# A fused two-block kernel: the shift of the last feed-forward stage taken out of the matmuls and summed on VectorE in the stage before

## The chip, the cores and the metric

The kernel runs as one program on one core of a Trainium2 chip. The metric is the device time of one execution in microseconds (us). A profile is one execution taken by the hardware profiler; its times start at the first instruction.

## The reference, cut to what matters

Two transformer blocks follow each other. The second has two layers over a context of 256 tokens and a latent of 512 tokens, width 1024, with a modulation computed from a condition vector. Only the end of its second layer is touched:

```
def modulate(x, g, shift, scale):
    return rmsnorm_2(x, g) * (1 + scale) + shift

def swiglu(h, w_in, w_out):
    g, u = jnp.split(h @ w_in, 2, axis=-1)
    return (jax.nn.silu(g) * u) @ w_out
...
x = x + g2 * rmsnorm_2(swiglu(modulate(x, norm_g[l, 2], sh2, sc2), ffn_w_in[l], ffn_w_out[l]), norm_g[l, 3])
```

`w_in` is 1024 x 5632 (22 groups of 128 gate columns and 22 of up columns, D_FF_2 = 2816), `w_out` 2816 x 1024. Everything is float32. For l = 1 (the last layer) only the 512 latent tokens are computed here. Since a norm's factor is one number per token, `modulate(x) @ w` is `r * ((x * g * (1 + scale)) @ w) + shift @ w`: the last term is one number per output row, the same for all tokens. The kernel works with it in this form.

## The kernel before, in words

Activations lie transposed: 128 channels on the partitions, tokens along the free axis. A float32 product is made of three fp32r matmuls, high x high, low x high and high x low parts, so every operand is split into a `hi` copy (ScalarE, L306) and a `lo` rest (VectorE, L307). `wload` fetches 128 x 1024 weights (512 KB) on SyncE's queue into one of three `raw` buffers (L303) and splits them into one of two `whi`/`wlo` pairs; it is written 300 places ahead of where it stands (`ahead`), so that weights come early.

`proj2` makes one projection: 8 steps k over the 1024 input channels, in each the three products for each segment of columns (`mm2`, matmul on L1020). The normalized but unscaled activations are in `hh` (hi) and `hl` (lo), [128, 8, 832] each. In a segment of 258 columns two columns hold the shift of latent and context: their product is `shift @ w`, which `ffn2` copies out of PSUM (L1656, L1664, 128 x 2) and adds as the bias of Silu (L355) and in L1669.

`ffn2(0, ...)`, called the first feed-forward stage below (layer 0, about 1737 to 2260 us), works on 768 tokens in segments of 258 and 512 columns. `ffn2(1, ...)`, the last one (about 2555 to 2912 us), works on 512 tokens in segments of 258 (`segl`: shift columns and latent tokens 0 to 255) and 256 columns. Either has 22 units of a gate and an up projection. The first two projections are made by `first2` (L980) in pieces while the stage before still ends, so 42 are left. Groups of 2, 4, 4, 4, 4 and 4 units are followed by their share of `w_out` (output tiles d, pairs of them in one weight load, 512 columns in one pass for the last stage); the last group is done by `sums` (L1616), 256 columns at a time, followed by `post`, which normalizes, adds the residual and stores.

The order on TensorE is the order in which the program is written. The other engines' order is laid out by a planner before the run. `tick` is called after each step k of a projection and each hidden tile of a down product; it advances side work (generators put in with `later`), which is how work is spread among the matmuls. Earlier, `ada_steps` already does such side work: it fetches 128 x 512 pieces (256 KB, tile `araw`, three buffers) during the first block's feed-forward stages and multiplies and sums each with two condition vectors in VectorE instructions with an accumulator (L869).

`lt`/`LT`/`LTB` say at which column of `hh` the latent tokens begin: 320 until the attention of layer 1, then 304. The arena of a stage has a fixed number of tile slots (`t`, 128 x 768): 25 in the first stage, 26 in the last.

Of the kernel before, what the change touches and what calls it, by code (L numbers as in the profile page):

```python
# [9 lines left out]
F32 = mybir.dt.float32  # L10
# [3 lines left out]
ALU = mybir.AluOpType  # L14
AX = mybir.AxisListType
PSUM = bass.MemoryType.PSUM

P = 128
S = 512
SC = 256  # L20
T2 = S + SC


CO, LT, HW = 16, 320, 832
LTB = 304
KD = 8
NF = 22
EPS = 1e-6
WU = 1024
# [125 lines left out]
def _pack_second(i):  # L155
    a = {}
    a["ctxT"] = np.ascontiguousarray(i["ctx_2"][0].T)

    a["ada"] = np.ascontiguousarray(i["ada_w_2"].transpose(0, 2, 1)).reshape(-1)
    a["cond"] = np.stack([i["c_2"][0], i["c_ctx_2"]])  # L160
    w = _Units("w2")
    wi = i["ab_w_in_2"][0]
    gc = [-1] * P
    for n, o in ((0, 0), (2, 32), (1, 64), (3, 96)):
        gc[o:o + 4] = _rng(4096 + 4 * n, 4)
    w.add("bg", _units(wi, [gc]))
    for h in range(4):
        w.add(("hg", h), _units(wi, [_rng(1536 + h * P), _rng(2048 + h * P), _rng(h * P), _rng(512 + h * P)]))
    w.add("bqk", _units(wi, [_rng(2560 + j * P) for j in range(4)]))
    w.add("bv", _units(wi, [_rng(3072 + h * P) for h in range(4)]))  # L170
    w.add("gate", _units(wi, [_rng(1024 + h * P) for h in range(4)] + [_rng(3584 + h * P) for h in range(4)]))
    w.add("abo", _units(i["ab_w_out_2"][0], [_rng(d * P) for d in range(KD)]))

    def ffn(l):
        wf = i["ffn_w_in_2"][l]
        _ffn(w, l, wf[:, :NF * P], wf[:, NF * P:], i["ffn_w_out_2"][l])

    ffn(0)
    perm = np.concatenate([np.arange(32), np.arange(64, 96), np.arange(32, 64), np.arange(96, P)])
    wq = i["attn_w_qkv_2"][0]  # L180
    w.add("ck", _units(wq, [8 * P + perm, 9 * P + perm]))
    w.add("cv", _units(wq, [_rng(10 * P), _rng(11 * P)]))
    w.add("cq", _units(wq, [h * P + perm for h in range(8)]))
    w.add("co", _units(i["attn_w_out_2"][0], [_rng(d * P) for d in range(KD)]))
    ffn(1)
    a["w2"] = w.array()
    gb = np.zeros((P, 1), np.float32)
    for n, o in ((0, 0), (2, 32), (1, 64), (3, 96)):
        gb[o:o + 4, 0] = i["ab_gate_b_2"][0, n]
    v = [_cols(i["ada_b_2"][l]) for l in range(2)]  # L190
    v += [_cols(i["norm_g_2"][l, n]) for l in range(2) for n in range(4)]
    v += [_cols(i["ab_conv_2"][0, n]) for n in range(3)]
    v += [gb]
    v += [_cols(i["hgrn_lb_2"][d, n]) for d in range(2) for n in range(3)]
    v += [_cols(i["ab_out_g_2"][0])]
    v += [_cols(i["attn_qk_g_2"][0, n][perm]) for n in range(2)]
    a["vec2"] = np.concatenate(v, axis=1)
    return a
# [61 lines left out]
class Body:  # L260
# [643 lines left out]
    def shift2(self, l, m, ctx=True, lat=False):  # L904

        sh = self.ada[l][:, m * 8:m * 8 + 8, :]
        for o in (CO + SC,) * ctx + (self.lt - 2,) * lat:
            self.split(self.hh[:, :, o:o + 2], self.hl[:, :, o:o + 2], sh)

    def squares2(self, k, x, o, w, acc, tmp=None):  # L910

# [12 lines left out]
    def feed2(self, k, x, o, w, l, n):  # L924

        for c, s in ((0, 1), (SC, 0)):
            a, b = max(o, c), min(o + w, (SC, T2)[1 - s])
            if a < b:
                h = a + (self.lt - SC, CO)[s]
                self.split_scaled(self.hh[:, k, h:h + b - a], self.hl[:, k, h:h + b - a], x[:, a - o:b - o],  # L930
                                  self.mod[l][n][:, k, s:s + 1])

# [12 lines left out]

    SEG = ((CO, SC + 2), (LT, S))

    @property
    def segl(self):
        return ((self.lt - 2, SC + 2), (self.lt + SC, SC))  # L950

    @property
    def partl(self):
        return ((0, 0, self.lt - 2, SC + 2), (1, 0, self.lt + SC, SC))

    def proj2(self, seg, key, u=0):

        if self.pre:
            return self.pre.pop(0)
        ps = self.mmtile()  # L960
        wh, wl = self.wload("w2", key, u)
        self.mm2(ps, wh, wl, 0, [(self.hh[:, k, :], self.hl[:, k, :]) for k in range(KD)], seg)
        return ps

    PART = ((0, 0, CO, SC + 2), (1, 0, LT, SC), (1, SC, LT + SC, SC))

    def first2(self, parts, units, pend):
# [670 lines left out]
    def ffn2(self, l, r, seg, lat, parts, acc, post):  # L1638

        nc = self.nc  # L1640
        ys = [None] * KD
        if lat:
            cols = ((slice(SC, 2 * SC), 0, 2, 0), (slice(2 * SC, T2), 1, 0, 0))
            bcol = slice(0, 2)
            hseg, outs = ((SC, S),), ((slice(SC, T2), 0),)
        else:
            cols = ((slice(0, SC), 0, 0, 1), (slice(SC, T2), 1, 0, 0))
            bcol = slice(SC, SC + 2)
            hseg, outs = self.SEGM, ((slice(0, SC), 0), (slice(SC, T2), 1))
        hid = []  # L1650

        def unit(f):
            pg = self.proj2(seg, ("f", l, f), 0)
            a = self.T()
            bg = self.small(2)
            nc.vector.tensor_copy(bg, pg[:, 0, bcol])  # L1656
            for c, b, p0, s in cols:
                n = c.stop - c.start
                nc.vector.tensor_tensor(a[:, c], pg[:, b, p0:p0 + n], r[:, c], ALU.mult)
                self.act(a[:, c], a[:, c], AF.Silu, bias=bg[:, s:s + 1])  # L1660
            pu = self.proj2(seg, ("f", l, f), 1)
            u = self.T()
            bu = self.small(2)
            nc.vector.tensor_copy(bu, pu[:, 0, bcol])  # L1664
            hi, lo = self.T(F32R), self.T(F32R)
            for c, b, p0, s in cols:
                n = c.stop - c.start
                nc.vector.tensor_tensor(u[:, c], pu[:, b, p0:p0 + n], r[:, c], ALU.mult)
                nc.vector.scalar_tensor_tensor(a[:, c], u[:, c], bu[:, s:s + 1], a[:, c], ALU.add, ALU.mult)  # L1669
                self.split(hi[:, c], lo[:, c], a[:, c])  # L1670
            hid.append((hi, lo, 0, 0))

        f = 0
        for gi, g in enumerate(GROUPS):
# [6 lines left out]
            for d in range(0, KD, 2):  # L1681
                wh, wl = self.wload("w2", ("d", l, gi), d // 2, 2 * g * P)
                for i in range(2):
                    ps = self.mmtile() if len(hseg) > 1 else Banks(self.aux())
                    self.mm2(ps, wh, wl, i * g * P, hid[:g], hseg)
                    k = d + i
# [8 lines left out]
            del hid[:g]  # L1695
        if not lat:
            self.shift2(1, 0, lat=True)
        W = []
        for o, w in parts:
            for d in range(0, KD, 2):  # L1700
# [16 lines left out]
    def mixer_c(self, r):  # L1717
        nc = self.nc
# [72 lines left out]
            lag(rest)  # L1791

        def qproj(h):
            ps = self.proj2(self.segl, "cq", h)
            z = T()
            b = self.small(2)
            nc.vector.tensor_copy(b, ps[:, 0, 0:2])
            nc.vector.tensor_tensor(z[:, :SC], ps[:, 0, 2:SC + 2], r[:, SC:2 * SC], ALU.mult)
            nc.vector.tensor_tensor(z[:, SC:], ps[:, 1, :SC], r[:, 2 * SC:T2], ALU.mult)
            nc.scalar.activation(z, z, AF.Identity, bias=b[:, 0:1])  # L1800
            sqs = squares(z, S)
            hi, lo = T(F32R), T(F32R)
            qs.append((hi, lo))

            def rest():
                headnorm(z, sqs, S, 0)
                rope(z)
                self.split(hi, lo, z)
            lag(rest)
# [4 lines left out]
        held = []  # L1814

        def store(h, o):
            hc = slice(LTB, LTB + S)
            self.split(self.hh[:, h, hc], self.hl[:, h, hc], o)

        def attend(h, qp):  # L1820
# [54 lines left out]
        for n in range(2 * 16 + 4):  # L1875
# [7 lines left out]
                store(*held.pop(0))  # L1883
            if n == 1 or n % 4 == 0 and 0 < n <= 20:
                late.pop(0)()
        return [(self.hh[:, h, :], self.hl[:, h, :], CO, LTB - SC) for h in range(8)]

    def arena(self, name, slots, width=784):
        es = ExitStack()
# [5 lines left out]
    def second_begin(self):  # L1895

        nc, tc = self.nc, self.tc
        self.e2 = ExitStack()
        pb = self.e2.enter_context(tc.tile_pool(name="blk2", bufs=1, reuse_waits="tile"))
        self.dr = self.e2.enter_context(tc.tile_pool(name="dram", bufs=1, space=bass.MemoryType.DRAM))  # L1900
        self.lt = LT
        self.hh = pb.tile([P, KD, HW], F32R, tag="hh", name="hh")
        self.hl = pb.tile([P, KD, HW], F32R, tag="hl", name="hl")
        self.accs = [pb.tile([P, T2], F32, tag=f"acc{i}", name=f"acc2{i}") for i in range(2)]
# [1 line left out]
        p = es.enter_context(tc.tile_pool(name="ctx0", bufs=1, reuse_waits="tile"))  # L1906
# [9 lines left out]
    def second(self, xall, pf, hb, acc, ef, eb):  # L1916

        nc, tc = self.nc, self.tc
# [14 lines left out]
        def leave(o, tail):  # L1933
            c = slice(o, o + SC)
            v, r = self.stats1(pf, acc, c, tail)
            for k in range(KD):
# [38 lines left out]
        self.drain()  # L1975
        ea.close()

        ea = self.arena("ffn20", 25, T2)
        self.ffn2(0, n0, self.SEG, False, ((0, SC), (SC, SC), (S, SC)), na,
                  lambda ys, o, w: self.post(ys, 0, o, w, na, self.mod[0][3], feed(1, 0), n0))  # L1980
        self.first2(self.PART, (("ck", 0), ("ck", 1)), norms)
# [4 lines left out]

        ea = self.arena("mixc", 20, S)
        mix = self.mixer_c(n0)
        self.lt = LTB
        self.lo_eng = nc.vector  # L1990
        ea.close()

        ex = self.residual(SC)
        nc.sync.dma_start(self.xr, spill[1])
        ea = self.arena("out1", 14, T2)
        self.shift2(1, 3, ctx=False, lat=True)
        self.out2("co", mix, ((SC, SC), (S, SC)), SC, na,
                  lambda ys, o, w: self.post(ys, SC, o, w, na, self.mod[1][1], feed(1, 2), n0))
        self.first2(self.partl, ((("f", 1, 0), 0), (("f", 1, 0), 1)), norms[1:])
        self.drain()  # L2000
        ea.close()

# [2 lines left out]
        def store(k, x, o, w):  # L2005
            if k % 2:
# [1 line left out]
                dst = self.out[(k - 1) * P:(k + 1) * P, o - SC:o - SC + w]  # L2008
                nc.sync.dma_start(dst.rearrange("(k p) s -> p k s", p=P), src)

        self.ffn2(1, n0, self.segl, True, ((SC, SC), (S, SC)), na,
                  lambda ys, o, w: self.post(ys, 0, o, w, na, self.mod[1][3], store))
        self.drain()
        ea.close()
# [28 lines left out]
```

## Time and profile before

| | us |
|---|---|
| median of 3 runs | 2936.16 |
| the three runs | 2933.27, 2936.16, 2939.81 |
| the profiled execution, its own time | 2936.96 |
| span of that profile, first to last instruction | 2934.9 |

PE is TensorE's matmuls, PEld its weight loads, DVE VectorE, ACT ScalarE, POOL GpSimd, SP SyncE; SPq is SyncE's queue of DMA issues. A busy share is read for a stretch, not for the whole. PEclk is the granted TensorE clock, 1.00 being 2.4 GHz.

### The profile page before, as it was taken

What the parts mean: (1) busy time and instruction counts of PE and PEld (TensorE: products, weight loads), DVE (VectorE), ACT (ScalarE), POOL (GpSimd) and SP (SyncE); (2) the same over time, 40 slices, a digit from 0 to 9 for tenths busy, and PEclk for the clock granted to TensorE, in tenths of its full rate; (3) what the DMA queues carried; (4) which work ended last, traced back from release to release, by engine and by line L of the source; (5) the groups of instructions that cost most, each with busy time, mean ns of one, the idle gap of its engine ahead of it and who ended that gap; (6) DMA issues with size and microseconds to landing.
All of it is one profiled execution on the core that took longest, in us unless ns stands there. A gap on an engine that the chain in (4) does not pass through costs nothing. (4 is left out here: it accounts for less than half of the span.)

```text
span 2934.9 us, 42299 instructions
## 1 busy us (share of the span) xinstructions
PE 2819.5 (96%) x16554; PEld 2464.0 (84%) x16554; DVE 1861.5 (63%) x3532; ACT 1197.4 (41%) x2090; POOL 565.6 (19%) x437
## 2 busy tenths in 40 slices
PE   9999999999999999999999989999999899999997
PEld 7777888877778888878877888888888888899997
DVE  7679995476689994768545463343335687544445
ACT  5663222255642223554354453122214577532223
POOL 3631000037410000534342230000003320300002
PEclk9999999999999999999999999999999999999998
DMA  4235663232156653211121312222222211133332
GB/s 145 76 94 173 201 197 115 93 104 69 58 164 203 196 188 101 87 39 49 44 80 51 101 29 72 65 65 65 59 64 65 80 37 54 56 101 94 94 94 72
DMA packets 98936, 278.46 MB, mean 95 GB/s; under 512 B 11505, under 2 KB 16881, under 8 KB 98225
## 3 DMA queue, kind: packets, MB, share of 16 engines
q1 hardware_dynamic: 98736, 275.76, 29.9%
q8 instruction: 130, 2.13, 0.3%
q14 instruction: 70, 0.57, 0.1%
HBM read 264.84 MB, written 6.68 MB: 93 GB/s over the span
## 5 line engine op out<-in xcount | busy, mean ns | idle before, releaser
L306 ACT ACTIVATE whi<-raw 128x1024 fp32r<-128x1024 f32 (+1 forms) x363 | 378.0, 1042 | 1199.1 <-PE b L1020 423.6
L1020 PE MATMUL b<-hh,whi 128*128 128x258 f32 (+1 forms) x2000 | 544.7, 321 | 0.0
L1020 PE MATMUL b<-hh,wlo 128*128 128x258 f32 x2000 | 468.7, 315 | 0.0
L1020 PE MATMUL b<-hl,whi 128*128 128x258 f32 (+1 forms) x2000 | 467.0, 315 | 0.0
L307 DVE TENSOR_TENSOR wlo<-raw,whi 128x1024 fp32r<-128x1024 f32 (+1 forms) x321 | 391.2, 1219 | 105.3 <-ACT whi L306 104.4
L1020 PEld LDWEIGHTS b<-hh,whi 128*128 128x128 f32 x2000 | 369.5, 189 | 26.8 <-issue 3.9
L1020 PEld LDWEIGHTS b<-hh,wlo 128*128 128x128 f32 x2000 | 351.7, 189 | 24.4
L1020 PEld LDWEIGHTS b<-hl,whi 128*128 128x128 f32 x2000 | 347.9, 189 | 24.8
L334 PE MATMUL b<-hbl,whi 128*128 128x512 f32 x704 | 275.2, 391 | 2.6 <-DVE hbl L345 2.6
L333 PE MATMUL b<-hbh,whi 128*128 128x512 f32 x704 | 275.8, 392 | 1.0 <-ACT hbh L344 1.0
L869 DVE SCALAR_TENSOR_TENSOR junk<-araw,cond 128x512 f32<-128x512 f32 x384 | 271.2, 706 | 7.7 <-ACT cond L355 2.2
L335 PE MATMUL b<-hbh,wlo 128*128 128x512 f32 x704 | 275.1, 391 | 0.3 <-DVE wlo L307 0.3
L1601 POOL TENSOR_TENSOR acc<-acc,t 128x256 f32<-128x256 f32 (+1 forms) x54 | 48.9, 906 | 1002.1 <-ACT t L1596 1001.3
L1020 PE MATMUL b<-t,whi 128*128 128x256 f32 (+1 forms) x864 | 213.5, 356 | 0.0
L392 POOL TENSOR_TENSOR acc<-acc,sq 128x512 f32<-128x512 f32 (+1 forms) x33 | 47.4, 1438 | 761.7 <-ACT sq L389 761.1
L1020 PEld LDWEIGHTS b<-t,whi 128*128 128x128 f32 x864 | 151.7, 188 | 23.6
L334 PEld LDWEIGHTS b<-hbl,whi 128*128 128x128 f32 x704 | 132.8, 189 | 31.3 <-DVE hbl L345 3.3
L333 PEld LDWEIGHTS b<-hbh,whi 128*128 128x128 f32 x704 | 132.7, 189 | 29.3 <-ACT hbh L344 1.4
L335 PEld LDWEIGHTS b<-hbh,wlo 128*128 128x128 f32 x704 | 132.8, 189 | 28.8 <-DVE wlo L307 1.0
L307 POOL TENSOR_TENSOR wlo<-raw,whi 128x1024 fp32r<-128x1024 f32 x42 | 106.4, 2535 | 168.6 <-ACT whi L306 137.6
L335 PE MATMUL b<-hidh,wlo 128*128 128x512 f32 (+1 forms) x352 | 134.1, 381 | 1.2 <-DVE wlo L307 1.1
L333 PE MATMUL b<-hidh,whi 128*128 128x512 f32 (+1 forms) x352 | 133.7, 380 | 0.0
(454 smaller groups left out, 5741.1 us busy)
## 6 DMA issues: line engine op xcount, KB each, us to landing
raw<-w SPq DMA_DIRECT2D x365, 512.0 KB, 3.5
araw<-ada SPq DMA_DIRECT2D x192, 256.0 KB, 3.1
raw<-w SPq DMA_DIRECT2D x18, 256.0 KB, 2.7
xr<-xd SPq DMA_DIRECT2D x2, 2048.0 KB, 8.2
t<-dm SPq DMA_DIRECT2D x8, 384.0 KB, 5.0
x<-xT SPq DMA_DIRECT2D x8, 256.0 KB, 4.8
kTh<-krh SPq DMA_DIRECT2D x32, 64.0 KB, 2.0
kTl<-krl SPq DMA_DIRECT2D x32, 64.0 KB, 2.0
```

The source lines that it names most:

```text
L306: self.last = nc.scalar.activation(hi[:, :m], r, AF.Copy).ins
L307: self.lo_eng.tensor_tensor(lo[:, :m], r, hi[:, :m].bitcast(F32), ALU.subtract)
L333: t.matmul(out, ah, bh, start=start, stop=False, skip_group_check=True)
L334: t.matmul(out, ah, bl, start=False, stop=False, skip_group_check=True)
L335: t.matmul(out, al, bh, start=False, stop=stop, skip_group_check=True)
L392: nc.gpsimd.tensor_tensor(acc[:, c], acc[:, c], t[:, c], ALU.add)
L869: nc.vector.scalar_tensor_tensor(junk, raw, 1.0, self.cond[:, s, k], ALU.mult, ALU.mult, accum_out=self.adah[:, i, t, s:s + 1])
L1020: t.matmul(ps[:, b, :w_], w[:, s], x[:, o:o + w_], start=(k == 0 and b not in seen), stop=(k == n - 1 and i == 2), skip_group_check=True)
L1601: nc.gpsimd.tensor_tensor(ac, ac, t, ALU.add)
```

## The change

The shift of the last feed-forward stage no longer goes through the matmuls. A generator, `shift_sums`, is put among the matmuls of the first feed-forward stage. At its first turn it writes the shift vector (1024 values) to DRAM and reads it back broadcast to all partitions (`sh`). Then, for each of the 44 groups of 128 rows of the transposed `w_in` (a new input `wt`), it fetches four pieces of 128 x 256 (128 KB, tile `sraw`, two buffers), one at every second turn; one VectorE instruction with an accumulator multiplies a piece by its part of the vector and sums it, and a `tensor_reduce` adds the four sums. The 44 columns lie where the modulation of layer 0 was (`shsum`).

The last stage then has one segment of 512 columns in one PSUM bank: three matmuls a step where there were six. The copies of the shift product from PSUM fall away there, the elementwise work takes 512 columns at a time, the two projections of `first2` have 256 columns in both halves, and the write of the shift columns (`shift2(1, 3)`) goes. The latent tokens stay at column 320 throughout. The first stage's arena has 24 slots instead of 25; small `pad` tiles are added.

```
-LTB = 304
...
+    a["wt"] = np.ascontiguousarray(i["ffn_w_in_2"][1].T).reshape(-1)
...
+    def shift_sums(self):
+
+        nc = self.nc
+        sr = self.dr.tile([1, WU], F32, tag="sr", name="sr")
+        nc.sync.dma_start(sr.rearrange("o (k p) -> p (o k)", p=P), self.ada[1][:, 24:32, 0])
+        sh = self.ar.tile([P, WU], F32, tag="sh", name="sh")
+        nc.sync.dma_start(sh, sr.partition_broadcast(P).rearrange("q o k -> q (o k)"))
+
+        self.shsum = self.ada[0].rearrange("p t s -> p (t s)")
+        yield
+        for t in range(2 * NF):
+            rows = self.ap["wt"][t * P * WU:(t + 1) * P * WU].rearrange("(p k) -> p k", p=P)
+            part = self.small(4)
+            for i in range(4):
+                k = slice(i * SC, i * SC + SC)
+                raw = self.ar.tile([P, SC], F32, tag="sraw", bufs=2, name=self.nm("sraw"))
+                nc.sync.dma_start(raw, rows[:, k])
+                nc.vector.scalar_tensor_tensor(raw, raw, 1.0, sh[:, k], ALU.mult, ALU.mult, accum_out=part[:, i:i + 1])
+                yield
+                yield
+            nc.vector.tensor_reduce(self.shsum[:, t:t + 1], part, AX.X, ALU.add)
...
+    SEGL = ((LT - 2, SC + 2), (LT + SC, SC))
+    SEGS = ((LT, S),)
...
-        ps = self.mmtile()
+        ps = self.mmtile() if len(seg) > 1 else Banks(self.aux())
...
+    PARTS = ((0, 0, LT, SC), (0, SC, LT + SC, SC))
...
         if lat:
-            cols = ((slice(SC, 2 * SC), 0, 2, 0), (slice(2 * SC, T2), 1, 0, 0))
-            bcol = slice(0, 2)
+            cols = ((slice(SC, T2), 0, 0, 0),)
...
-            bg = self.small(2)
-            nc.vector.tensor_copy(bg, pg[:, 0, bcol])
+            if lat:
+                bg, bu = self.shsum[:, f:f + 1], self.shsum[:, NF + f:NF + f + 1]
+            else:
+                bg, bu = self.small(2), self.small(2)
+                nc.vector.tensor_copy(bg, pg[:, 0, bcol])
...
+        self.ar.tile([P, 16], F32, tag="pad", name=self.nm("pad"))
...
-        ea = self.arena("ffn20", 25, T2)
+        ea = self.arena("ffn20", 24, T2)
+        self.later(self.shift_sums(), 0)
...
-        self.shift2(1, 3, ctx=False, lat=True)
+        self.ar.tile([P, 16], F32, tag="pad", name="pad1")
...
-        self.first2(self.partl, ((("f", 1, 0), 0), (("f", 1, 0), 1)), norms[1:])
+        self.first2(self.PARTS, ((("f", 1, 0), 0), (("f", 1, 0), 1)), norms[1:])
...
-        self.ffn2(1, n0, self.segl, True, ((SC, SC), (S, SC)), na,
+        self.ffn2(1, n0, self.SEGS, True, ((SC, SC), (S, SC)), na,
```

## Rows read from the trace of the kernel before

**Rows 1.** The page, part 1: engine, busy us, share, instructions.

```profile
PE 2819.5 (96%) x16554; PEld 2464.0 (84%) x16554; DVE 1861.5 (63%) x3532; ACT 1197.4 (41%) x2090; POOL 565.6 (19%) x437
```

**Rows 2.** Windows: us; busy (count) of PE, PEld, DVE, ACT, POOL; PEclk; DMA share; GB/s.

```profile
300.00:400.00 100.00, 100.00 (x443) 82.81 (x442) 94.65 (x213) 28.40 (x33) 0.00 (x0) 1.00 0.64 202
...
2000.00:2100.00 100.00, 100.00 (x575) 87.88 (x575) 38.55 (x69) 20.53 (x28) 0.00 (x0) 1.00 0.21 64
...
2600.00:2650.00 50.00, 50.00 (x360) 47.30 (x359) 25.60 (x51) 15.22 (x23) 0.00 (x0) 1.00 0.30 93
```

**Rows 3.** Waits of all engines, 2560 to 2885 us: total, times, longest.

```profile
ACT whi L306 <- PE b L1020: 145.1, 40, 4.6
...
DVE sml L1664 <- PE b L1020: 70.3, 20, 4.3
```

**Rows 4.** Timeline of TensorE, last stage: start us, us, instruction, count.

```profile
2656.04 0.28 PE L1020 MATMUL b<-hh,whi 128*128 128x256 f32 x1
...
2656.39 0.28 PE L1020 MATMUL b<-hh,whi 128*128 128x258 f32 x1
...
2701.70 0.63 PE L1020 MATMUL b<-t,whi 128*128 128x512 f32 x2
...
2723.47 0.28 PE L1020 MATMUL b<-hh,whi 128*128 128x256 f32 x1
```

**Rows 5.** Timeline of TensorE, first stage: two steps k of a projection.

```profile
2001.08 0.51 PE L1020 MATMUL b<-hh,whi 128*128 128x258 f32 x2
...
2002.12 0.51 PE L1020 MATMUL b<-hh,whi 128*128 128x258 f32 x2
```

**Rows 6.** Line L869, all of it: duration ns min/median/max, first and last start.

```profile
L869 DVE SCALAR_TENSOR_TENSOR junk<-araw,cond x384: 676/685/1790, 194.3 to 1093.9; 128x512 f32<-128x512 f32 x192
L869 DVE DVE_READ_ACCUMULATOR junk<-araw,cond x384: 75/81/88, 194.9 to 1094.5; 128x1 f32 x192
```

**Rows 7.** VectorE by line and form, 1800 to 2100 us: busy, mean ns, idle before.

```profile
L1669 DVE SCALAR_TENSOR_TENSOR t<-t,sml,t 128x512 f32<-128x512 f32 x12 | 8.9, 744 | 0.0
...
L1669 DVE SCALAR_TENSOR_TENSOR t<-t,sml,t 128x256 f32<-128x256 f32 x11 | 5.2, 475 | 0.0
...
L1664 DVE COPY sml<-b 128x2 f32<-128x2 f32 x12 | 1.9, 159 | 72.9 <-PE b L1020 72.9
```

**Rows 8.** DMA issues of the whole span: count, KB each, median us to landing.

```profile
raw<-w SPq DMA_DIRECT2D x365, 512.0 KB, 3.5
araw<-ada SPq DMA_DIRECT2D x192, 256.0 KB, 3.1
...
kTh<-krh SPq DMA_DIRECT2D x32, 64.0 KB, 2.0
...
t<-cnt SPq DMA_DIRECT2D x4, 256.0 KB, 3.7
cx<-ctxT SPq DMA_DIRECT2D x8, 128.0 KB, 2.7
xr<-ctxT SPq DMA_DIRECT2D x1, 1024.0 KB, 12.2
```

**Rows 9.** Waits of SyncE's queue, 1790 to 2230 us.

```profile
SPq L303 <- DVE wlo L307: 416.3, 53, 8.3
```

**Rows 10.** Tile araw: the DMA issues, and VectorE's idle time before L869.

```profile
L866 SPq DMA_DIRECT2D araw<-ada x192: 327/328/1236, 186.9 to 1088.1; - x192
...
  DMA araw<-ada: 0.2, 1
```

**Rows 11.** Timelines of ScalarE and VectorE, first stage: one weight split to the next.

```profile
1998.90 1.06 ACT L306 ACTIVATE whi<-raw 128x1024 fp32r<-128x1024 f32 x1 [6.30 <-issue]
...
2007.22 1.06 ACT L306 ACTIVATE whi<-raw 128x1024 fp32r<-128x1024 f32 x1 [4.30 <-PE b L1020]
...
2000.37 1.22 DVE L307 TENSOR_TENSOR wlo<-raw,whi 128x1024 fp32r<-128x1024 f32 x1
```

More of the change, by code (lines that the diff above doesn't have):

```diff
@@ L906, in shift2 @@
         sh = self.ada[l][:, m * 8:m * 8 + 8, :]
-        for o in (CO + SC,) * ctx + (self.lt - 2,) * lat:
+        for o in (CO + SC,) * ctx + (LT - 2,) * lat:
             self.split(self.hh[:, :, o:o + 2], self.hl[:, :, o:o + 2], sh)
+    def shift_sums(self):
[17 more added lines that the diff above has]
+            nc.vector.tensor_reduce(self.shsum[:, t:t + 1], part, AX.X, ALU.add)
     def squares2(self, k, x, o, w, acc, tmp=None):
@@ L928, in feed2 @@
             if a < b:
-                h = a + (self.lt - SC, CO)[s]
+                h = a + (LT - SC, CO)[s]
                 self.split_scaled(self.hh[:, k, h:h + b - a], self.hl[:, k, h:h + b - a], x[:, a - o:b - o],
@@ L946 @@
     SEG = ((CO, SC + 2), (LT, S))
[L948 to L954, printed above, removed]
+    SEGL = ((LT - 2, SC + 2), (LT + SC, SC))
+    SEGS = ((LT, S),)
     def proj2(self, seg, key, u=0):
@@ L1662, in unit @@
             u = self.T()
-            bu = self.small(2)
-            nc.vector.tensor_copy(bu, pu[:, 0, bcol])
+            if not lat:
+                nc.vector.tensor_copy(bu, pu[:, 0, bcol])
             hi, lo = self.T(F32R), self.T(F32R)
@@ L1793, in qproj @@
         def qproj(h):
-            ps = self.proj2(self.segl, "cq", h)
+            ps = self.proj2(self.SEGL, "cq", h)
             z = T()
@@ L1816, in store @@
         def store(h, o):
-            hc = slice(LTB, LTB + S)
+            hc = slice(LT, LT + S)
             self.split(self.hh[:, h, hc], self.hl[:, h, hc], o)
@@ L1885, in mixer_c @@
                 late.pop(0)()
-        return [(self.hh[:, h, :], self.hl[:, h, :], CO, LTB - SC) for h in range(8)]
+        return [(self.hh[:, h, :], self.hl[:, h, :], CO, LT - SC) for h in range(8)]
     def arena(self, name, slots, width=784):
@@ L1900, in second_begin @@
         self.dr = self.e2.enter_context(tc.tile_pool(name="dram", bufs=1, space=bass.MemoryType.DRAM))
-        self.lt = LT
         self.hh = pb.tile([P, KD, HW], F32R, tag="hh", name="hh")
@@ L1988, in second @@
         mix = self.mixer_c(n0)
-        self.lt = LTB
         self.lo_eng = nc.vector
```

## The prediction

> **What bounds the kernel now.** I read the page's first part, then the windows by stage, the waits, and TensorE's timeline in the two stages. The page shows TensorE busy for 96% of the span [rows 1], but that alone doesn't say that shorter matmul work is shorter time, so the stages decide. In the last feed-forward stage TensorE is busy in 50.00 of 50 us, at full clock, with VectorE at 25.6 and ScalarE at 15.2 [rows 2]. The waits of that stage have no row of TensorE; the long ones are ScalarE and VectorE waiting for TensorE [rows 3]. So TensorE's pace sets that stage, and a nanosecond taken off its steps is a nanosecond of the kernel. In the first feed-forward stage it is the same: 100.00 of 100 us, VectorE at 38.55 [rows 2]. There the change adds work, all off TensorE; the question is whether that stays hidden.
>
> **The last stage: pass for pass.** One gain carries the forecast. TensorE's timeline shows a stretch of eight projections from 2656.04 to 2701.70 us, 64 steps of six matmuls (three of 258, three of 256 columns): 45.66 / 64 = 0.7134 us a step. Right behind it the down products of the same stage run from 2701.70 to 2723.47, 8 output tiles x 4 hidden tiles = 32 steps of three matmuls of 512 columns, in the order that the changed projections will have (whi, whi, wlo): 21.77 / 32 = 0.6803 us a step [rows 4]. So a step of the changed projection should take 0.6803 instead of 0.7134, 0.0331 less. 42 projections x 8 steps = 336 steps, 336 x 0.0331 = 11.1 us.
>
> Where it comes from: the columns are 514 against 512 a pair, at 2.4 GHz 0.8 ns of the 11.0 ns saved per pair; the rest is a fixed part of each matmul. A pair takes 0.7134 / 3 = 237.8 ns, 23.6 above its 514 columns; one pass of 512 takes 226.8 ns, 13.5 above its columns. One instruction instead of two drops about ten.
>
> The Trainium skill ("TensorE: Matmul & The Clock Gate", Back-to-back issue gap) puts a warm back-to-back gap at N/2.4 plus 2.5 ns. By it a pair would save only 0.8 + 2.5 = 3.3 ns, 336 x 3 x 3.3 = 3.4 us in all, an estimate from that page. The trace's fixed part is four to five times as large at both widths, so I keep the rows.
>
> **Smaller edits of the last stage.** The 44 shift copies (159 ns each [rows 7]), the second instruction of each elementwise pair and `shift2(1, 3)` are VectorE and ScalarE work, both of which wait for TensorE there [rows 3]: nothing. The two projections of `first2` lose two columns in 48 matmuls, 48 x 2 / 2.4 = 40 ns: nothing. Weights are needed every 8 x 0.680 = 5.44 us instead of 5.71; the stretch with side work at 300 to 400 us, where projections also have 512 columns, keeps TensorE busy 100.00 of 100 us while SyncE carries twice the bytes (202 GB/s against 93) [rows 2]. So no weight should be late.
>
> **The first stage: what is added, and under what it hides.** A step of its projections takes 2002.12 − 2001.08 = 1.04 us [rows 5]. The generator yields once and then 44 x 4 x 2 = 352 times; the stage has 42 x 8 + 18 x 8 + 96 = 576 turns, so the pieces fill about 353 x 1.04 = 367 us of it, one piece every 2.08 us.
>
> VectorE: a row sum over 512 columns takes 685 ns and 81 ns for reading the accumulator [rows 6]; the trace has none over 256. From L1669, which costs 744 at 512 and 475 at 256 columns [rows 7], 256 columns fewer are worth 269 ns: 416 + 81 = about 500 ns. Bounds: 269 from below (the columns alone), 766 from above (the 512-column price). 176 x 0.50 = 88 us, plus 44 small reductions at the price of the 128 x 2 copy, 7 us: 95 us in 367, which lifts VectorE from 38.6% to about 65% (upper bound 77%). At 300 to 400 us VectorE is busy 94.65 of 100 with such sums and TensorE still 100.00 [rows 2]. So I cost it at nothing; the work that hides it is 8.3 us of matmuls a projection. Without cover it would be up to 95 us.
>
> SyncE: 178 more issues at 0.33 us [rows 10] = 58 us on a queue that in this stage stands 416 of 440 us waiting for a `raw` buffer [rows 9]. What queues behind a piece's wait is the next weight load. Three `raw` buffers and two split pairs hold what TensorE uses in several times 8.3 us, and both waits are released by VectorE's order. Nothing. The transfers: 44 x 512 KB = 23.1 MB in 367 us, 63 GB/s on top of 64; the stretch at 300 to 400 us carries 202 [rows 2]. Nothing.
>
> Start of the generator: the shift vector goes out in 1024 runs of 4 bytes, comes back as a 512 KB broadcast, and only then can the first sum run. VectorE takes its instructions in order, so if the first sum stands too early in its order, everything behind it waits: the split of the next weights, and then TensorE. No row shows such a scatter; I bound it by the smallest landing, 2.0 us, and the longest, 12.2, the broadcast by 3.5 us of a load of its size, and the first piece by 2.0 to 2.7 [rows 8]: 7.5 to 18.4 us. The cover: a weight's split starts when TensorE turns to the next projection (1998.90), `wlo` is done at 2001.59, and it is needed when ScalarE's next copy is released at 2007.22 [rows 11], 5.6 us later. Price: 7.5 − 5.6 = 1.9 to 18.4 − 5.6 = 12.8 us if the first sum stands at once in the order, zero if the planner lets it wait as long as the transfers take. I take zero and keep 12.8.
>
> The Trainium skill ("DMA: Bandwidth & Descriptors", Specifications) says that transfers under 512 bytes are read-modify-write. The scatter's runs of 4 bytes fall under that; no run here shows it yet, and it speaks for the long end of the bound.
>
> One slot fewer (24): the live tiles at the fullest are 8 outputs, 10 hidden tiles and two at work, 20. Nothing.
>
> Sum: the profiled execution took 2936.96 us; 2936.96 − 11.1 = 2925.9. The median of the runs is 0.8 lower, so 2925.1, rounded to **2925**.
>
> **Rivals.**
>
> *The fixed part isn't saved (same).* The 512-column pace is read on down products, with other operands. If a 512-column pass over `hh` cost the fixed part of two, only two columns in 514 would go, 336 x 3 x 0.8 ns = 0.8 us, and the time would be 2935.4. Against it: in rows 4 the two patterns stand side by side at the same clock. The formula of "TensorE: Matmul & The Clock Gate" in the Trainium skill, named above, would give 2936.2 − 3.4 = 2932.8, an estimate on the same side.
>
> *The start stalls (faster to same).* As priced: 2925 + 1.9 to 2925 + 12.8 = 2927 to 2938, deciding from 5.2 us of stall on. Against it: it happens once.
>
> *Two buffers are too few (slower).* A piece's buffer is loaded again only when its sum is done, so two pieces take one landing, a sum of 0.50 and an issue of 0.33. With two pieces due in 4.16 us the landing may be 3.3 us. From there on VectorE falls behind at every pair, its order being fixed, and takes the drains and weight splits with it; TensorE then goes at VectorE's pace. At the 3.7 us that one 256 KB load shows [rows 8] it is 88 x 0.4 = 35 us, 2960; the gain is used up at 88 x 0.13 = 11, a landing of 3.43 us. For it: a weight load of 512 KB takes 3.5 us and shares the queue. Against it: loads of 64 and 128 KB land in 2.0 and 2.7 [rows 8], three `araw` buffers made VectorE wait 0.2 us in all [rows 10], and VectorE has a third of its time free to catch up.
>
> **How the numbers follow.** Forecast 0.72, fixed part not saved 0.05, a start stall that counts 0.12, two buffers 0.08, something else on the slow side 0.03. About 0.2% (5.9 us) is what a measurement of this kernel can tell from no change, so faster means under 2930.3. The forecast's own range is 2921 to 2929: the three runs of before lie 2.9 below to 3.7 above their median, and the rows' price is good to a few tenths. With the start stalls up to 2935 about 0.83 is held. Faster: 0.72 and a third of the start stalls, 0.76. Same: the unsaved fixed part and the other stalls, 0.13. Slower: 0.11.
>
> **What would show it.** Right: eight projections of the last stage take 64 x 0.680 = 43.5 us instead of 45.66, in 512-column matmuls of 227 ns start to start; no TensorE wait in the first stage; VectorE there at about 65%; `sraw` landing under 3 us. Wrong: idle time of TensorE on `wlo` or a PSUM bank in the first stage, VectorE idle before row sums for a DMA over and over, a long gap at the start of that stage, or a 512-column step well above 0.68 us.

## The result and the profile after

The changed kernel takes 2959.17 us in the median (four runs, 2958.5 to 2965.03) against 2936.93 for the kernel before: 1.0087 times the time, interval 1.0075 to 1.0099. It is slower by 22 us where 12 us less were forecast, and lies outside the range. The profiled execution spans 2957.3 us against 2934.9.

The gain came as forecast, and more was lost elsewhere. TensorE's timeline after the change (start us, us, instruction, count) at the two ends of the first feed-forward stage, of eight projections of the last stage, and of the last stage:

```profile
1731.13 0.69 PE L1039 MATMUL b<-hh,whi 128*128 128x258 f32 x2
...
2267.01 0.40 PE L1635 MATMUL b<-t,whi 128*128 128x256 f32 x2
...
2588.36 0.58 PE L1039 MATMUL b<-hh,whi 128*128 128x512 f32 x1
...
2621.22 0.39 PE L1039 MATMUL b<-hh,whi 128*128 128x512 f32 x1
...
2664.74 0.62 PE L1039 MATMUL b<-t,whi 128*128 128x512 f32 x2
...
2914.98 0.40 PE L1635 MATMUL b<-t,whi 128*128 128x256 f32 x2
```

and the same borders of these stages in the kernel before:

```profile
1730.89 0.69 PE L1020 MATMUL b<-hh,whi 128*128 128x258 f32 x2
...
2233.29 0.40 PE L1616 MATMUL b<-t,whi 128*128 128x256 f32 x2
...
2554.69 0.47 PE L1020 MATMUL b<-hh,whi 128*128 128x256 f32 x1
...
2892.58 0.39 PE L1616 MATMUL b<-t,whi 128*128 128x256 f32 x2
```

Eight projections of the last stage take 2664.74 − 2621.22 = 43.52 us, 0.680 a step, where they took 45.66 [rows 4]. The last stage up to its last group takes 326.62 us instead of 337.89: 11.3 us gained. The first stage up to its last group takes 535.88 instead of 502.40: 33.5 us lost. Between the two stages, and behind them, nothing changed (321.4 us both times, then 42.3 both times). 33.5 − 11.3 = 22.2, nearly all of the 22.4 us between the spans.

The windows of the first stage with side work, and after it (us; busy and count of PE, PEld, DVE, ACT, POOL; PEclk; DMA share; GB/s), and TensorE's waits in that stage:

```profile
1850.00:1900.00 50.00, 44.89 (x250) 37.98 (x249) 31.41 (x101) 9.48 (x12) 0.00 (x0) 1.00 0.43 134
2100.00:2150.00 50.00, 50.00 (x291) 44.13 (x290) 17.45 (x29) 9.45 (x12) 0.00 (x0) 1.00 0.19 64
...
PE b L1039 <- DVE wlo L308: 24.4, 18, 4.2
```

TensorE, never idle there before [rows 2], now stands for 5 of 50 us, waiting for the low part of the weights. Yet VectorE is busy for only 31.4 of 50. So it wasn't short of time; it stood still with work behind it.

These waits, 24.4 us, are not the whole 33.5. In four short stretches of this stage TensorE was granted half its clock (0.50, which is 1.2 GHz), and in the kernel before in none. Each lies at or right behind a wait of TensorE, though not every wait has one. The window of one of them (us; the columns as above), and TensorE's timeline in it and behind it:

```profile
1899.80:1903.21 3.41, 3.01 (x10) 2.63 (x11) 2.05 (x7) 0.00 (x0) 0.00 (x0) 0.50 0.61 181
...
1900.20 1.01 PE L1039 MATMUL b<-hh,wlo 128*128 128x258 f32 x2 [2.27 <-DVE wlo L308]
1901.01 0.84 PE L1039 MATMUL b<-hh,whi 128*128 128x258 f32 x2
1901.65 0.84 PE L1039 MATMUL b<-hl,whi 128*128 128x258 f32 x2
...
1903.78 0.51 PE L1039 MATMUL b<-hh,wlo 128*128 128x258 f32 x2
1904.12 0.51 PE L1039 MATMUL b<-hh,whi 128*128 128x258 f32 x2
```

A pair of matmuls takes 0.64 us in this stretch and 0.34 behind it. Over the four stretches (13.7 us, with about 13 of matmuls) that is some 6 us, an estimate from these two paces. About 3 us of the loss stay unexplained.

What VectorE stood still for is told by the view of the tile `sraw` (durations in ns min/median/max, first and last start):

```profile
L927 SPq DMA_DIRECT2D sraw<-wt x176: 327/328/1764, 1730.9 to 2021.5; - x176
L928 DVE SCALAR_TENSOR_TENSOR sraw<-sraw,sh x176: 412/425/428, 1735.3 to 2023.7; 128x256 f32<-128x256 f32 x176
L928 DVE DVE_READ_ACCUMULATOR sraw<-sraw,sh x176: 76/83/86, 1735.7 to 2024.0; 128x1 f32 x176
its engine sat idle before it (us, times) until:
  DMA sraw<-wt: 122.7, 93
...
DMA to landing us min/median/max: 2.0/2.3/5.0
```

The two instructions of a sum take 425 and 83 ns, near what was forecast, and a piece lands in 2.3 us in the median. (The two overlap: the next timeline has the second start 0.35 us after the first, so that both end together and a sum holds VectorE for about 0.43 us.) But VectorE stood 122.7 us before the sums, and the 176 sums were over at 2023.7, not at 1731 + 367 = 2098: one every 1.65 us, not every 2.08. VectorE's timeline between two weight splits shows the rest:

```profile
1860.16 1.22 DVE L308 TENSOR_TENSOR wlo<-raw,whi 128x1024 fp32r<-128x1024 f32 x1
...
1862.00 0.43 DVE L928 SCALAR_TENSOR_TENSOR sraw<-sraw,sh 128x256 f32<-128x256 f32 x1 [0.55 <-DMA sraw<-wt]
1862.35 0.08 DVE L928 DVE_READ_ACCUMULATOR sraw<-sraw,sh 128x1 f32 x1
1862.59 0.43 DVE L928 SCALAR_TENSOR_TENSOR sraw<-sraw,sh 128x256 f32<-128x256 f32 x1 [0.15 <-DMA sraw<-wt]
1862.94 0.08 DVE L928 DVE_READ_ACCUMULATOR sraw<-sraw,sh 128x1 f32 x1
1865.62 0.43 DVE L928 SCALAR_TENSOR_TENSOR sraw<-sraw,sh 128x256 f32<-128x256 f32 x1 [2.60 <-DMA sraw<-wt]
1865.97 0.08 DVE L928 DVE_READ_ACCUMULATOR sraw<-sraw,sh 128x1 f32 x1
1866.89 0.42 DVE L928 SCALAR_TENSOR_TENSOR sraw<-sraw,sh 128x256 f32<-128x256 f32 x1 [0.85 <-DMA sraw<-wt]
...
1868.19 0.43 DVE L928 SCALAR_TENSOR_TENSOR sraw<-sraw,sh 128x256 f32<-128x256 f32 x1 [0.39 <-DMA sraw<-wt]
...
1869.59 0.42 DVE L928 SCALAR_TENSOR_TENSOR sraw<-sraw,sh 128x256 f32<-128x256 f32 x1 [0.37 <-DMA sraw<-wt]
...
1870.34 1.22 DVE L308 TENSOR_TENSOR wlo<-raw,whi 128x1024 fp32r<-128x1024 f32 x1
```

From one split to the next 10.2 us pass where TensorE needs 8.3; six sums stand between the two, and before each VectorE waits for a piece, 4.9 us in all. At the end TensorE waits:

```profile
1871.61 0.61 PE L1039 MATMUL b<-t,wlo 128*128 128x256 f32 x2 [1.58 <-DVE wlo L308]
```

Six, where the turns give four (eight turns a projection, a piece at every second): the order of VectorE's instructions in the built program, which the traces show too, has this many sums between one low part and the next:

```
kernel after           6 6 6 7 2 2 4 2 6 6 6 6 6 6 6 6 5 6 6 6 6 6 6 6 6 6 6 6 5 6 6 5
four to a split (e2)   6 6 4 2 2 2 2 2 6 4 4 4 ... 4
one buffer (e5)        3 3 3 4 1 2 2 1 3 3 3 3 ... 3 1
```

Nothing ties a piece to a matmul, since neither its load nor its sum reads anything that TensorE makes. A turn is only a place in the written program. With one, two and four buffers the planner put mostly three, six and ten sums between two splits (e5, this kernel, e6), so it seems to have taken them as early as it reckoned a buffer to be free; its own reckoning is in no trace.

### The profile page after: what moved, and what is told of

It reads as the page before. It is cut to its first block, busy times and chain, and to the rows that moved or that the text cites. A ratio compares the mean times of both kernels' runs of the same rounds, so it can differ in the third digit from the quotient of the medians.

```text
span 2957.3 us, 40893 instructions
## 1 busy us (share of the span) xinstructions
PE 2818.6 (95%) x15546; PEld 2418.5 (82%) x15546; DVE 1927.7 (65%) x3795; ACT 1190.3 (40%) x2045; POOL 563.2 (19%) x437
## 5 line engine op out<-in xcount | busy, mean ns | idle before, releaser
L1039 PE MATMUL b<-hh,whi 128*128 128x512 f32 (+2 forms) x1664 | 487.0, 352 | 0.0
L1039 PE MATMUL b<-hh,wlo 128*128 128x512 f32 (+2 forms) x1664 | 466.8, 346 | 14.2 <-DVE wlo L308 14.2
L1039 PE MATMUL b<-hl,whi 128*128 128x512 f32 (+2 forms) x1664 | 465.0, 345 | 0.0
L1039 PEld LDWEIGHTS b<-hh,wlo 128*128 128x128 f32 x1664 | 310.9, 190 | 55.4 <-DVE wlo L308 17.9
L1039 PEld LDWEIGHTS b<-hl,whi 128*128 128x128 f32 x1664 | 311.6, 190 | 38.1
L1039 PEld LDWEIGHTS b<-hh,whi 128*128 128x128 f32 x1664 | 308.5, 190 | 40.2 <-issue 3.9
L1039 PE MATMUL b<-t,whi 128*128 128x256 f32 (+1 forms) x864 | 213.4, 356 | 0.0
L1039 PEld LDWEIGHTS b<-t,whi 128*128 128x128 f32 x864 | 153.1, 189 | 23.8
L335 PEld LDWEIGHTS b<-hbl,whi 128*128 128x128 f32 x704 | 132.8, 189 | 31.4 <-DVE hbl L346 3.3
L928 DVE SCALAR_TENSOR_TENSOR sraw<-sraw,sh 128x256 f32<-128x256 f32 x176 | 73.0, 423 | 124.0 <-DMA sraw<-wt 122.7
L1039 PE MATMUL b<-t,wlo 128*128 128x512 f32 (+1 forms) x432 | 130.8, 358 | 10.2 <-DVE wlo L308 10.2
```

The costliest lines, as they stand in the source:

```text
L335: t.matmul(out, ah, bl, start=False, stop=False, skip_group_check=True)
L928: nc.vector.scalar_tensor_tensor(raw, raw, 1.0, sh[:, k], ALU.mult, ALU.mult, accum_out=part[:, i:i + 1])
L1039: t.matmul(ps[:, b, :w_], w[:, s], x[:, o:o + w_], start=(k == 0 and b not in seen), stop=(k == n - 1 and i == 2), skip_group_check=True)
```

## The experiments

All are edits of the changed kernel. The theories that the expectations name: A, VectorE's order and the two buffers; B, VectorE's added work as such; C, the added transfers; D, the slot fewer or the moved tiles. Theory F, that the number of sums between two splits counts whatever the buffers, came up after the first four runs. Measured against the kernel before, run beside them (2935.8 to 2937.2 us):

| run | median us | ratio, interval | first stage, us |
|---|---|---|---|
| changed kernel | 2959.17 | 1.0087 (1.0075 to 1.0099) | 535.9 |
| e1 the 512-column pass only | 2923.62 | 0.9945 (0.9927 to 0.9963) | 502.4 |
| e2 four to a split | 2925.70 | 0.9958 (0.9942 to 0.9974) | 502.4 |
| e3 sums without loads | 2923.12 | 0.9948 (0.9933 to 0.9963) | 502.4 |
| e4 loads without sums | 2925.62 | 0.9960 (0.9947 to 0.9973) | 502.4 |
| e5 one buffer | 2999.82 | 1.0223 (1.0203 to 1.0243) | 571.6 |
| e6 four buffers | 2940.08 | 1.0026 (1.0015 to 1.0036) | 520.3 |
| e7 five to a split | 2964.91 | 1.0102 (1.0083 to 1.0121) | 540.5 |
| e8 four buffers, four to a split | 2924.47 | 0.9962 (0.9949 to 0.9975) | 502.4 |
| e9 four buffers, six to a split | 2922.92 | 0.9958 (0.9942 to 0.9974) | 502.4 |
| e10 four buffers, five to a split | 2925.68 | 0.9958 (0.9945 to 0.9972) | 502.4 |
| e11 as e8, more rounds | 2926.04 | 0.9961 (0.9948 to 0.9974) | 502.4 |

The last column is read as above, from the first matmul of L1039 in the stage to the first of its last group (their numbers shift with the edits).

**e1, the pass alone.**

```
-        self.later(self.shift_sums(), 0)
+        self.shsum = self.ada[0].rearrange("p t s -> p (t s)")
```

> The row sums and their transfers are left out (the bias is whatever lies in the old modulation's place); the one 512-column pass, 24 slots and the tile places stay. Theory A (the planner put six pieces between two weight splits, where the turns would give four; with two buffers a pair of pieces takes 3.3 us on the chip, three pairs 9.9 us against 8.3 us of matmuls, and VectorE's order holds TensorE up): the last stage's gain alone is left, 2936.9 - 11.3 = 2925.6. Theory B (VectorE's added work as such delays TensorE): 2925.6. Theory C (the added transfers and SyncE issues make the weight loads late): 2925.6. Theory D (24 slots instead of 25, or the moved tiles, hold the first stage up): still about 2959.

2923.62 us. This kernel leaves the shift sums out. The gain stands alone when the side work goes, and the first stage is as long as before: theory D is out.

**e2, four to a split.** `last_lo` is the instruction that made the last low part of weights on VectorE; `issue_after` only orders instructions on one engine.

```
-                nc.vector.scalar_tensor_tensor(raw, raw, 1.0, sh[:, k], ALU.mult, ALU.mult, accum_out=part[:, i:i + 1])
+                with self.tc.issue_after(self.last_lo):
+                    nc.vector.scalar_tensor_tensor(raw, raw, 1.0, sh[:, k], ALU.mult, ALU.mult, accum_out=part[:, i:i + 1])
```

> Each row sum is queued on VectorE behind the low part of the weights that were loaded at that place of the program, so that the planner can't put more than about four pieces between two splits; two buffers, all the work of the change. Theory A: two pairs take 6.6 us of 8.3, no VectorE idle time that TensorE feels, 2925.6 (2923 to 2929). Theories B, C, D: the same work, the same transfers, the same slots, so 2950 to 2960.

2925.70 us with all the work of the change. The window has TensorE busy all the time at a VectorE load of 59%:

```profile
1800.00:1900.00 100.00, 100.00 (x575) 87.87 (x574) 58.68 (x179) 20.63 (x28) 0.00 (x0) 1.00 0.39 128
```

The same instructions and bytes cost 33 us in one order and nothing in the other: B and C fall as explanations of the loss. The sums now run at about the forecast's pace, 176 of them from 1737.1 to 2091.3 us, one every 2.02 us.

**e3, sums without loads, and e4, loads without sums.** e3 multiplies the resident vector by itself, with six to a split held by `issue_after` as in e2 and this spacing; e4 leaves the sums out and queues the loads behind the weight loads in the same way.

```
+                    nc.vector.scalar_tensor_tensor(raw, sh[:, k], 1.0, sh[:, k], ALU.mult, ALU.mult, accum_out=part[:, i:i + 1])
+                n += 1
                 yield
-                yield
+                if n % 3 == 0:
+                    yield
```

> The row sums stay, six between two splits as in the changed kernel, but take both operands from the resident vector: no piece is loaded, so the sums are not those of the reference. Theory A: nothing to wait for, VectorE has 6 x 0.5 + 3.2 = 6.2 us of work in 8.3, 2925.6 (to 2930 where the first splits have eight to ten). Theory B: 2950 to 2960. Theory C: 2925.6. Theory D: 2959.

> The 176 pieces are loaded into the two buffers, about six between two weight loads, but not summed (the bias is left out of the computation). Theory A: VectorE waits for no piece; a pair of loads takes some 2.7 us without the sum, three pairs 8.1 of 8.3 us, so 2926 to 2932. Theory C: the same bytes and issues, 2950 to 2960. Theory B: 2925.6. Theory D: 2959.

2923.12 and 2925.62 us, the second 0.4 us under A's range. Neither half costs anything alone, at mostly six to a split; the loss needs sums that wait for their loads.

**e5, one buffer, and e6, four buffers,** with nothing queued by hand (e6 with 23 slots, for room).

```
-tag="sraw", bufs=2,
+tag="sraw", bufs=1,      (e5)
+tag="sraw", bufs=4,      (e6)
```

> The changed kernel with one buffer for the pieces instead of two, nothing queued by hand; the planner then puts three pieces between two weight splits, over 58 splits instead of 31. Theory A (the loop of load, landing and sum, slower on the chip than the planner took it): three single rounds of 3.3 us, 9.9 us a split as before, now over nearly twice as many splits: the first stage 502 + 33.5 x 58 / 31 = 565 us, the kernel 2925.6 + 63 = 2988 (2975 to 3000). Theory F (what hurts is how many pieces stand between two splits): three instead of six, no loss, 2925.6.

> The changed kernel with four buffers and 23 slots, nothing queued by hand; the planner then puts mostly ten pieces between two splits. Theory A: ten pieces are two and a half rounds of four buffers, 2.5 x 3.3 = 8.25 us of 8.32, at the limit, over some 18 splits, and VectorE has 10 x 0.5 + 3.2 = 8.2 us of work: 2926 to 2938. Theory F: ten instead of six, a loss per split larger than the 1.1 us of the changed kernel, 2950 or more.

e5: 2999.82 us, at the upper end of what A expected. Only three sums stand between two splits now, so by F nothing should be lost, but the first stage lost 69 us, 1.13 a split over the 61 stretches between splits that the built order has (1.05 over 32 in the changed kernel; the expectation had counted 58 and 31). The view of the tile shows VectorE waiting for 128 of the 176 pieces:

```profile
  DMA sraw<-wt: 299.8, 128
...
DMA to landing us min/median/max: 2.0/2.1/4.6
```

e6: 2940.08, 2 us above A's range and 10 below F's least. With more buffers the planner only ran further ahead, mostly ten to a split, and the first stage lost 17.9 us over 20 stretches, 0.9 each. VectorE waits 44.3 us for pieces in all. That waits and not the work of ten sums are the cause here is likely, but e6 alone doesn't show it.

**e7, five to a split, two buffers.** As e2, with three second turns in five pieces (`if n % 5 in (0, 2, 4): yield`).

> Two buffers, the pieces queued behind the low parts of the weights, five to a split instead of four. Theory A: 2.5 rounds of 3.3 us, 8.25 of 8.32 us, just inside: 2925.6 to 2931. Theory F: between four (2925.7) and six (2959.2), about 2942.

2964.91 us: a miss, 34 us above the upper end of A and 23 above F. The linear account, 2.5 rounds of 3.3 us, doesn't hold. The timelines of SyncE's queue and of VectorE in e7 over one split show why:

```profile
1959.37 0.33 SPq L304 DMA_DIRECT2D raw<-w  x1
1959.81 7.16 SPq L930 DMA_DIRECT2D sraw<-wt  x5
...
1958.13 1.21 DVE L308 TENSOR_TENSOR wlo<-raw,whi 128x1024 fp32r<-128x1024 f32 x1
1959.26 0.42 DVE L932 SCALAR_TENSOR_TENSOR sraw<-sraw,sh 128x256 f32<-128x256 f32 x1
...
1959.60 0.42 DVE L932 SCALAR_TENSOR_TENSOR sraw<-sraw,sh 128x256 f32<-128x256 f32 x1
...
1963.54 0.43 DVE L932 SCALAR_TENSOR_TENSOR sraw<-sraw,sh 128x256 f32<-128x256 f32 x1 [3.50 <-DMA sraw<-wt]
...
1963.89 0.42 DVE L932 SCALAR_TENSOR_TENSOR sraw<-sraw,sh 128x256 f32<-128x256 f32 x1
...
1966.19 0.43 DVE L932 SCALAR_TENSOR_TENSOR sraw<-sraw,sh 128x256 f32<-128x256 f32 x1 [1.68 <-DMA sraw<-wt]
...
1967.93 1.22 DVE L308 TENSOR_TENSOR wlo<-raw,whi 128x1024 fp32r<-128x1024 f32 x1
```

Two pieces lie ready at the split. The third is loaded into a buffer that the first frees, behind the 512 KB weight load that the split itself freed on SyncE's queue, and VectorE waits 3.50 us; the fifth needs a trip more, 1.68 us of waiting, before the next split may run. The split comes 9.8 us after the last. In e2, with four to a split, only one trip stands between two splits, and the time up to it is filled with other work:

```profile
1951.52 1.22 DVE L308 TENSOR_TENSOR wlo<-raw,whi 128x1024 fp32r<-128x1024 f32 x1
1952.65 0.42 DVE L931 SCALAR_TENSOR_TENSOR sraw<-sraw,sh 128x256 f32<-128x256 f32 x1
...
1956.71 0.42 DVE L931 SCALAR_TENSOR_TENSOR sraw<-sraw,sh 128x256 f32<-128x256 f32 x1 [0.73 <-DMA sraw<-wt]
...
1958.59 1.02 DVE L1718 TENSOR_TENSOR t<-t,b 128x256 f32<-128x256 f32 x2 [0.91 <-PE b L1042]
1959.61 1.23 DVE L308 TENSOR_TENSOR wlo<-raw,whi 128x1024 fp32r<-128x1024 f32 x1
```

There VectorE even waits 0.91 us for TensorE before the next split. So what counts is how many trips of a load stand open between two splits: one with four pieces, two or more with five or six. Theory A holds in its mechanism, with whole trips in place of a rate. That this count decides was read from these two timelines; the runs with four buffers below test it.

**e9 and e10, six and five to a split again, but with four buffers** (`issue_after` and spacing as in e3 and e7, with the loads; 23 slots).

> Six pieces between two splits as in the changed kernel, queued by hand so that the number stays, but four buffers and 23 slots. Theory A (VectorE's fixed order with too few buffers leaves trips of a load open between two splits): four pieces are loaded ahead, the open trips are covered, 2925 to 2929 (a few splits at the start have nine). Theory F (six pieces between two splits are too many, whatever the buffers): 2950 to 2960.

> The run with five to a split that lost 39 us against four, with four buffers and 23 slots instead of two and 24. Theory A: 2925 to 2928, and VectorE's idle time for pieces falls from 150 us to under 40. Theory F: 2955 to 2965.

2922.92 and 2925.68 us. In e9 the number of sums between two splits is that of the changed kernel (up to nine in the first ones), and the loss is gone with two more buffers: F falls. The sums even run closer here, in 232.5 us against 288.3, so neither their pace nor that of the transfers is the cause. VectorE's wait for pieces, in the view of the tile of e9:

```profile
  DMA sraw<-wt: 43.2, 30
```

a third of the changed kernel's, and none of it felt by TensorE. For e10 it is 55.7 us, above the 40 that was expected, and no more felt.

**e8 and e11, the version to keep:** four buffers, 23 slots, four to a split.

> As the run with four to a split, with four buffers and 23 slots. Theory A: TensorE already waits for nothing there, so more buffers bring nothing: 2925.6, while VectorE's idle time before the sums falls from 88 us to under 40.

> The version with four buffers and four to a split once more, in more rounds: 2924 to 2926, ratio to the kernel before 0.996.

2924.47 and 2926.04 us. VectorE waits 0.8 us for pieces in e8, under the 40 that was expected. The ratios are 0.9962 and 0.9961: some 10 to 11 us below the kernel before and 33 to 35 below the changed one, like e2, e9 and e10. They can't be told from each other, nor from e1, which has no side work at all, and the first stage takes 502.4 us in each: as far as these runs can tell, the side work is then hidden entirely.

## Why the prediction was wrong

- **The last stage's gain was right.** 11.1 us were priced, 11.3 measured; a step is 0.680 us. The rival in which the fixed part isn't saved is out, and so is the 3.4 us by the Trainium skill's formula ("TensorE: Matmul & The Clock Gate", Back-to-back issue gap). The prediction took that formula for the pace of a stream, but the section gives it for an isolated matmul, and for a stream of weight loads and matmuls about 131 ns at 512 columns. These fp32r matmuls took 0.680 / 3 = 226.7 ns, so the trace's own pace decided.
- **The step that failed is "so the pieces fill about 353 x 1.04 = 367 us of it, one piece every 2.08 us".** It took the place of a piece in the written program for its place in VectorE's order. The planner put six between two splits, not four, and the order, once laid, holds on the chip whether the loads have landed or not. One sum came every 1.65 us, and the first stage took 33.5 us more. With four between two splits, one every 2.02 us, the kernel takes 2925.70 us, as forecast (e2).
- **The rival "two buffers are too few" named the place and the sign, and its price of 2960 was near the 2959.2, but that was luck: the figure in it was wrong.** It was to decide from a landing of 3.43 us on, and the landing is 2.3. With the pieces at the turns it would have cost nothing (e2). It took 8 of 100 because the due time came from the step above.
- **"VectorE has a third of its time free to catch up" was right as a share and wrong as a cover.** It had 19 of 50 us free, but its waits stood in its own order, ahead of the weight split. The stretch with `araw` [rows 2, 10] was no proof of cover: there the loads came in time (0.2 us of waiting in all), while here VectorE waited 122.7 us for them.
- **The price of VectorE's work was too high, which changed nothing.** The prediction added the accumulator's 81 ns to a sum, but rows 6 have it start 0.6 us into an instruction of 0.685, so it is almost all counted twice. VectorE is busy for 265.7 us in the first stage (1731 to 2267) instead of 195.2 (1731 to 2233): 70.5 us more, where 95 were priced. In e2 its load is 58.7%, not 65. TensorE feels neither this work nor the transfers (e2, e3, e4).
- **The start of the generator cost nothing, as taken.** TensorE's first wait in the stage ends at 1773.9 us, when the sums have run for 38 us, and with the same start nothing is lost in e2. The planner moved the scatter of the shift vector up to 1097 us, 630 us ahead of its use, and the broadcast landed in 4.6 us. The scatter itself took this long (KB, us to landing):

```profile
sr<-ada SPq DMA_DIRECT2D x1, 4.0 KB, 11.2
```

- **The slot fewer** cost nothing (e1).

What stays open is how long the planner took a load to be. Six sums, three rounds of two buffers, in 8.3 us and three rounds of one buffer in e5 would fit some 2.8 us a round, where the chip needs (2023.7 − 1735.3) / 175 x 2 = 3.3 and a first trip behind a weight load longer; the planner's own figures are in no trace.

## What to carry to other kernels

Work spread among matmuls in the written program is not spread on an engine whose order a planner lays out, unless something ties it to them: look at the order of the built program, and queue side work behind an instruction that keeps the pace. Count the loads that must land between two instructions that the bounding engine needs, and give side work so many buffers that none of these trips stands open there. An engine that is 60% busy can hold up another if its waits are in front of what the other needs.

## What the runs showed of the hardware

A 4 KB write to DRAM in 1024 runs of 4 bytes took 11.2 us to land, where 64 KB loads take 2.0 [rows 8] and the 256 KB writes of the output 2.2 (`outT<-xr`). The Trainium skill ("DMA: Bandwidth & Descriptors", Specifications) has transfers under 512 bytes as read-modify-write; this row agrees that such runs are slow, though not why.

A 128 KB load lands in 2.3 us in the median of the changed kernel, but in 3.5 in e8. There SyncE's queue issues four of them right behind each 512 KB weight load, as its timeline shows (start us, us, instruction, count):

```profile
1951.47 0.33 SPq L304 DMA_DIRECT2D raw<-w  x1
1951.89 2.08 SPq L929 DMA_DIRECT2D sraw<-wt  x4
```

The changed kernel has both: from 1800 to 2020 us its first piece behind a weight load lands in 3.35 us in the median, the third to the sixth in 2.1 to 2.3. The longer landings of e8 cost nothing; the shorter ones of the changed kernel did.

TensorE's clock fell where TensorE had been made to wait. In the first feed-forward stage it was granted 0.50 in four short stretches of the changed kernel, in eight of e5, two of e6 and four of e7; in the other runs, where TensorE doesn't wait there, in none. So some of these waits cost more than their own length.
